# A rotary embedding on one core: batch 0 stored whole, behind all five first loads

## The chip, the cores and the metric

The kernel runs on one core of a Trainium2 chip. The metric is the time of one execution on the device in microseconds (us). It is shown as the median of several executions. One further execution was taken with the hardware profiler on; all durations of single instructions and transfers come from that one.

A core has compute engines that work side by side. This kernel uses three of them for arithmetic or for starting transfers: VectorE (DVE), which does all multiplications and additions; ScalarE (ACT), which does a few conversions; and GpSimd (POOL), which here only issues transfers. SyncE (SP) issues four further transfers. The transfers themselves are moved by 16 DMA engines, which the page sums up as one row. Transfers that POOL issues stand in the queue that the page calls q0 (software_dynamic), those of SP in q1 (hardware_dynamic).

## The reference

The input `x` has 8 batches of 2048 positions, 16 heads and 64 elements, in float32; `cos` and `sin` have 32 values for each position. The two halves of each head are rotated against each other:

```python
def reference(x, cos, sin):
    head_dim = x.shape[-1]                       # 64
    x1 = x[..., :head_dim // 2].copy()
    x2 = x[..., head_dim // 2:].copy()
    cos = cos[None, :, None, :].copy()
    sin = sin[None, :, None, :].copy()
    out1 = x1 * cos - x2 * sin
    out2 = x1 * sin + x2 * cos
    return np.concatenate([out1, out2], axis=-1).astype(np.float32)
```

## The kernel before

A batch is 2048 positions, laid over 128 partitions with J = 16 positions ("rows" below) in each. A row is 16 heads of 64 elements, 1024 in all, so a whole batch is 128 x 16384 elements: 8.39 MB in float32 in main memory, half of that in float16 on the chip. All arithmetic is in float16. The transfers convert: a load reads float32 from main memory and writes float16 to the chip, a store does the reverse. The page gives the sizes of these transfers on the float16 side (4096 KB for a batch).

`buf` (line 47) is one tile with five slots, and batch b lives in slot b % 5, where it is loaded, rotated in place and stored from. So batches 0 to 4 have a slot from the start, and batches 5, 6 and 7 need the slots of 0, 1 and 2, after these have been stored.

`load(b, n)` (lines 62 to 71) issues one transfer for n neighbouring batches. For batch 0 it leaves out the first JA = 2 rows. Those come through the tile `head` in float32, on SP's queue (line 41), and ACT converts them into the slot (line 106). `store(b, n, j0, j1)` (lines 73 to 81) issues one transfer for n batches, or for rows j0 to j1 of one batch. Both are issued by POOL, and `in_ring` (lines 51 to 60) chains them, so that POOL issues them in the order in which the code calls them; it adds no wait of its own. An instruction on POOL that waits, though, holds up all issues behind it.

`rotate(b, j0, j1)` (lines 83 to 100) is three DVE operations over the rows given: the halves swapped times sine into the temporary `v` (L92), the batch times cosine in place (L98), and the sum (L100). A store waits for the L100 of its rows. The first L92 of a batch waits for its load.

SP issues sin_f, head and cos_f at the start (lines 40, 41 and 45). ACT converts sine (two forms, lines 104 and 105), the two head rows (106) and cosine (110).

The order of work around the change: load(0) and load(1) are issued; the first two rows of batch 0 are rotated; row 0 is stored; load(2, 2) for batches 2 and 3, and load(4); the other 14 rows of batch 0 are rotated, and rows 1 to 15 stored; then batches 1 and 2 are rotated and stored one by one, and load(5, 2) and load(7) fill the slots that come free. load(5, 2) waits for the stores of batches 0 and 1, load(7) for that of batch 2. Later stores are store(3, 2), store(5, 2) and batch 7 in three parts, the last of which goes out in float32 through `head` on SP's queue.

Of the kernel before, what the change touches and what calls it, by code (L numbers as in the profile page):

```python
# [1 line left out]

# [4 lines left out]


@with_exitstack  # L10
def kernel(
    ctx: ExitStack,
    tc: tile.TileContext,
    x: bass.AP,
    cos: bass.AP,
    sin: bass.AP,
    out: bass.AP,
):
    nc = tc.nc
    f16 = mybir.dt.float16  # L20
    f32 = mybir.dt.float32

    B, S, H, D = x.shape
    Dh = D // 2
    P = nc.NUM_PARTITIONS
    J = S // P
    NBUF = 5

    const_pool = ctx.enter_context(tc.tile_pool(name="rope_const", bufs=1))
    io_pool = ctx.enter_context(tc.tile_pool(name="rope_io", bufs=1))  # L30
    tmp_pool = ctx.enter_context(tc.tile_pool(name="rope_tmp", bufs=1))

    JA = 2
    head = const_pool.tile([P, JA, H, D], f32)
    x0 = x[0].rearrange("(p j) h d -> p j (h d)", j=J)
    sin_f = const_pool.tile([P, J, Dh], f32)
    cos_f = const_pool.tile([P, J, Dh], f32)
    cos_h = const_pool.tile([P, J, Dh], f16)
    sin_h = const_pool.tile([P, J, D], f16)
    nc.sync.dma_start(out=sin_f, in_=sin.rearrange("(p j) d -> p j d", j=J))  # L40
    nc.sync.dma_start(  # L41
        out=head.rearrange("p j h d -> p (j h d)"),
        in_=x0[:, 0:JA, :].rearrange("p j f -> p (j f)"),
    )
    nc.sync.dma_start(out=cos_f, in_=cos.rearrange("(p j) d -> p j d", j=J))

    buf = io_pool.tile([P, NBUF, J, H, D], f16)

    ring = []

    def in_ring(dma):
        if ring:
            tc.add_manual_dep(
                dma.ins,
                ring[-1].ins.name,
                mybir.DependencyInfo(mybir.DependencyClass.NoSync, mybir.DependencyReason.DATA),
                reason="order of the ring",
            )
        ring.append(dma)
        return dma  # L60

    def load(b, n=1):
        k = b % NBUF
        if n == 1:
            j0 = JA if b == 0 else 0
            dst = buf[:, k, j0:J, :, :].rearrange("p j h d -> p (j h d)")
            src = x[b].rearrange("(p j) h d -> p j (h d)", j=J)[:, j0:J, :].rearrange("p j f -> p (j f)")
        else:
            dst = buf[:, k : k + n, :, :, :].rearrange("p b j h d -> p b (j h d)")
            src = x[b : b + n].rearrange("b (p j) h d -> p b (j h d)", j=J)  # L70
        in_ring(nc.gpsimd.dma_start(out=dst, in_=src))  # L71

    def store(b, n=1, j0=0, j1=J):
        k = b % NBUF
        if n == 1:
            src = buf[:, k, j0:j1, :, :].rearrange("p j h d -> p (j h d)")
            dst = out[b].rearrange("(p j) h d -> p j (h d)", j=J)[:, j0:j1, :].rearrange("p j f -> p (j f)")
        else:
            src = buf[:, k : k + n, :, :, :].rearrange("p b j h d -> p b (j h d)")
            dst = out[b : b + n].rearrange("b (p j) h d -> p b (j h d)", j=J)  # L80
        return in_ring(nc.gpsimd.dma_start(out=dst, in_=src))  # L81

    def rotate(b, j0=0, j1=J):
        v = tmp_pool.tile([P, J, H, D], f16)
        n = j1 - j0
        js = slice(j0, j1)
        xt = buf[:, b % NBUF, js, :, :]
        shape = [P, n, H, 2, Dh]
        sin_b = sin_h[:, js, :].rearrange("p j (e d) -> p j e d", e=2).unsqueeze(2).to_broadcast(shape)
        cos_b = cos_h[:, js, :].unsqueeze(2).to_broadcast([P, n, 2 * H, Dh])  # L90
        xe = xt.rearrange("p j h (e d) -> p j h e d", e=2)
        nc.vector.tensor_mul(  # L92
            out=v[:, js, :, :].rearrange("p j h (e d) -> p j h e d", e=2),
            in0=xe[:, :, :, ::-1, :],
            in1=sin_b,
        )
        xw = xt.rearrange("p j h (e d) -> p j (h e) d", d=Dh)
        nc.vector.tensor_mul(out=xw, in0=xw, in1=cos_b)  # L98
        xa = xt.rearrange("p j h d -> p (j h d)")
        nc.vector.tensor_add(out=xa, in0=xa, in1=v[:, js, :, :].rearrange("p j h d -> p (j h d)"))  # L100

    load(0)
    load(1)
    nc.scalar.copy(out=sin_h[:, :, Dh:D], in_=sin_f)  # L104
    nc.scalar.mul(out=sin_h[:, :, 0:Dh], in_=sin_f, mul=-1.0)  # L105
    nc.scalar.copy(  # L106
        out=buf[:, 0, 0:JA, :, :].rearrange("p j h d -> p (j h d)"),
        in_=head.rearrange("p j h d -> p (j h d)"),
    )
    nc.scalar.copy(out=cos_h, in_=cos_f)  # L110
    rotate(0, 0, JA)
    store(0, 1, 0, 1)
    load(2, 2)
    load(4)
    rotate(0, JA, J)
    store(0, 1, 1, J)
    rotate(1)
    store(1)
    rotate(2)
    store(2)  # L120
    load(5, 2)
    load(7)
    rotate(3)
    rotate(4)
    store(3, 2)
    rotate(5)
    rotate(6)
    store(5, 2)
    rotate(7)
    gate = store(7, 1, 0, 9)  # L130
    store(7, 1, 9, J - JA)
    last = buf[:, 7 % NBUF, J - JA : J, :, :].rearrange("p j h d -> p (j h d)")
    dst = out[B - 1].rearrange("(p j) h d -> p j (h d)", j=J)[:, J - JA : J, :].rearrange("p j f -> p (j f)")
    nc.scalar.copy(out=head.rearrange("p j h d -> p (j h d)"), in_=last)  # L134
    end = nc.sync.dma_start(out=dst, in_=head.rearrange("p j h d -> p (j h d)"))
    tc.add_manual_dep(
        end.ins,
        gate.ins.name,
        mybir.DependencyInfo(mybir.DependencyClass.Sync, mybir.DependencyReason.DATA),
        reason="the last rows go out behind this part",  # L140
    )


# [1 line left out]
_INS = ['x', 'cos', 'sin']  # L145
_OUTS = [((8, 2048, 16, 64), 'float32')]


# [23 lines left out]
```

## Time and profile before

| What | Value |
|---|---|
| median of 3 executions | 316.51 us (316.36 to 316.55) |
| the profiled execution | 316.6 us |
| its span (first to last recorded work) | 314.8 us |
| read from and written to main memory | 67.63 MB and 67.11 MB |
| DVE operation on a whole batch (128 x 16384) | 8.69 us |
| one issue on POOL, one batch / two batches | 0.54 to 0.6 us / 0.71 us |
| sin_f (256 KB), issue to landing | 2.7 us |
| head (1024 KB), issue to landing | 6.9 us |
| cos_f (256 KB), issue to landing | 24.4 us |

The span is cut into 40 equal slices on the page, and each digit of a row is the busy share of a slice in tenths. The same strip can be had for any window, and then a slice is a fortieth of the window. "From issue to landing" runs from the start of the issuing instruction to the completion of the transfer, so it holds the time that the transfer stood in its queue. A row of the table of stretches gives the stretch, its length, the busy time of DVE, ACT and POOL with the number of instructions, the granted TensorE clock (unused here), the share of the DMA engines, and the GB/s that they moved, counted on the side that is written: 200-odd for a load, which writes float16, is as much traffic on the float32 side as 400-odd for a store.

### The profile page before, as it was taken

The page shows a single profiled execution, that of the slowest core. Times are in us where ns is not written, and L with a number is a line of the kernel's source. Part 1 is how long each engine was busy: PE and PEld are TensorE (multiplying, and loading weights), DVE is VectorE, ACT ScalarE, POOL GpSimd, SP SyncE. Part 2 cuts the span into 40 slices and gives each one's busy share as a digit, 9 for nine tenths or more (in the row PEclk, how much of TensorE's full clock was granted, in tenths as well). Part 3 has the DMA queues.
Part 4 walks back from the last instruction along what each step waited for, and adds up shares of the span by engine and source line. Part 5 has one row for each costly group of instructions (what it writes and reads, how often), then busy time and mean ns, then how long its engine had stood idle before and what let it go on. Part 6 is the DMA issues. An engine that isn't in the chain of part 4 may idle for free.

```text
span 314.8 us, 115 instructions
## 1 busy us (share of the span) xinstructions
DVE 209.1 (66%) x27; ACT 6.8 (2%) x6; POOL 8.6 (3%) x18
## 2 busy tenths in 40 slices
DVE  0105999999499999999950000899999999910000
ACT  3200000000000000000000000000000000020000
POOL 1002000000000000000010000000000000010000
DMA  9899999999999899999999999999999999999998
GB/s 284 187 262 200 200 266 200 200 262 204 200 200 317 382 492 407 400 400 533 400 200 208 258 200 200 229 237 333 400 491 441 400 400 525 408 400 400 433 427 339
DMA packets 3104, 101.71 MB, mean 323 GB/s; under 512 B 288, under 2 KB 288, under 8 KB 672
## 3 DMA queue, kind: packets, MB, share of 16 engines
q0 software_dynamic: 2528, 99.09, 98.1%
q1 hardware_dynamic: 576, 2.62, 2.2%
HBM read 67.63 MB, written 67.11 MB: 428 GB/s over the span
## 4 chain that ended last, share of the span: by engine, by line
DVE 66%; another core or an unknown queue 13%; DMA 8%; ACT 1%; issue 0%; SPq 0%; DVEq 0%; ACTq 0%
DVE buf L98 22%; DVE buf L100 22%; DVE v L92 22%; DMA cos_f<-in_cos_dram 8%; ACT head L134 1%; ACT cos_h L110 0%; SPq L41 0%; SPq L40 0%; DVEq L92 0%; ACTq L134 0%
## 5 line engine op out<-in xcount | busy, mean ns | idle before, releaser
L92 DVE TENSOR_TENSOR v<-buf,sin_h 128x16384 f16<-128x16384 f16 (+2 forms) x9 | 69.7, 7744 | 51.4 <-DMA buf<-in_x_dram 41.2
L98 DVE TENSOR_TENSOR buf<-buf,cos_h 128x16384 f16<-128x16384 f16 (+2 forms) x9 | 69.7, 7744 | 15.8 <-ACT cos_h L110 15.5
L100 DVE TENSOR_TENSOR buf<-buf,v 128x16384 f16<-128x16384 f16 (+2 forms) x9 | 69.7, 7744 | 0.3
L81 POOL DMA_DIRECT2D out_dram<-buf x8 | 4.7, 586 | 219.4 <-DVE buf L100 219.4
L134 ACT CAST head<-buf 128x2048 f32<-128x2048 f16 x1 | 1.9, 1898 | 249.9 <-DVE buf L100 249.9
L71 POOL DMA_DIRECT2D buf<-in_x_dram x6 | 3.7, 628 | 49.7 <-DMA out_dram<-buf 48.9
L106 ACT CAST buf<-head 128x2048 f16<-128x2048 f32 x1 | 1.9, 1897 | 3.5 <-DMA head<-in_x_dram 3.5
L104 ACT ACT_TABLE_LOAD x1 | 1.3, 1283 | 0.7 <-PEq L156 0.7
L110 ACT CAST cos_h<-cos_f 128x512 f16<-128x512 f32 x1 | 0.6, 617 | 16.1 <-DMA cos_f<-in_cos_dram 16.1
L104 ACT CAST sin_h<-sin_f 128x512 f16<-128x512 f32 x1 | 0.6, 617 | 1.4 <-DMA sin_f<-in_sin_dram 1.4
L105 ACT ACTIVATE sin_h<-sin_f 128x512 f16<-128x512 f32 x1 | 0.6, 624 | 0.0
L156 POOL MEMSET const-float32-0.0<- 128x1 f32 x1 | 0.1, 100 | 0.2 <-issue 0.2
L156 POOL MEMSET const-bfloat16-1.0<- 128x1 bf16 x1 | 0.1, 103 | 0.0
L156 POOL MEMSET const-float32-1.0<- 128x1 f32 x1 | 0.1, 100 | 0.0
L156 POOL MEMSET const-uint8-127<- 128x1 uint8 x1 | 0.1, 100 | 0.0
## 6 DMA issues: line engine op xcount, KB each, us to landing
buf<-in_x_dram POOLq DMA_DIRECT2D x2, 8192.0 KB, 55.2
buf<-in_x_dram POOLq DMA_DIRECT2D x3, 4096.0 KB, 57.4
out_dram<-buf POOLq DMA_DIRECT2D x1, 7680.0 KB, 68.3
out_dram<-buf POOLq DMA_DIRECT2D x1, 4608.0 KB, 28.6
buf<-in_x_dram POOLq DMA_DIRECT2D x1, 3584.0 KB, 22.3
out_dram<-buf POOLq DMA_DIRECT2D x1, 2560.0 KB, 34.1
head<-in_x_dram SPq DMA_DIRECT2D x1, 1024.0 KB, 6.9
out_dram<-head SPq DMA_DIRECT2D x1, 1024.0 KB, 8.4
```

Source lines behind the costliest of these rows:

```text
L71: in_ring(nc.gpsimd.dma_start(out=dst, in_=src))
L81: return in_ring(nc.gpsimd.dma_start(out=dst, in_=src))
L92: nc.vector.tensor_mul(out=v[:, js, :, :].rearrange("p j h (e d) -> p j h e d", e=2), in0=xe[:, :, :, ::-1, :], in1=sin_b,)
L98: nc.vector.tensor_mul(out=xw, in0=xw, in1=cos_b)
L100: nc.vector.tensor_add(out=xa, in0=xa, in1=v[:, js, :, :].rearrange("p j h d -> p (j h d)"))
L104: nc.scalar.copy(out=sin_h[:, :, Dh:D], in_=sin_f)
L105: nc.scalar.mul(out=sin_h[:, :, 0:Dh], in_=sin_f, mul=-1.0)
L106: nc.scalar.copy(out=buf[:, 0, 0:JA, :, :].rearrange("p j h d -> p (j h d)"), in_=head.rearrange("p j h d -> p (j h d)"),)
L110: nc.scalar.copy(out=cos_h, in_=cos_f)
L134: nc.scalar.copy(out=head.rearrange("p j h d -> p (j h d)"), in_=last)
L156: nc = _bacc.Bacc("TRN2", target_bir_lowering=False, num_devices=1)
```

## The change

Batch 0 is no longer stored in two parts. The store of its row 0 is taken out, the store of rows 1 to 15 becomes one of all 16 rows, and load(2, 2) and load(4) are issued right behind load(0) and load(1). The rotation of batch 0 stays in two parts (two rows, then fourteen).

```diff
@@ -101,6 +101,8 @@
 
     load(0)
     load(1)
+    load(2, 2)
+    load(4)
     nc.scalar.copy(out=sin_h[:, :, Dh:D], in_=sin_f)
     nc.scalar.mul(out=sin_h[:, :, 0:Dh], in_=sin_f, mul=-1.0)
     nc.scalar.copy(
@@ -109,11 +111,8 @@
     )
     nc.scalar.copy(out=cos_h, in_=cos_f)
     rotate(0, 0, JA)
-    store(0, 1, 0, 1)
-    load(2, 2)
-    load(4)
     rotate(0, JA, J)
-    store(0, 1, 1, J)
+    store(0)
     rotate(1)
     store(1)
     rotate(2)
```

POOL's order of issues becomes load(0), load(1), load(2, 2), load(4), store(0), store(1), store(2), load(5, 2) and so on: 13 transfers in place of 14. The order on DVE, ACT and SP is the same. load(5, 2) waits for one store of batch 0 where it waited for two.

## The prediction

> **What bounds the kernel now.** I read the page first: shares of the span, the slices, the queues, the chain of waits.
>
> ```profile
> span 314.8 us, 115 instructions
> DVE 209.1 (66%) x27; ACT 6.8 (2%) x6; POOL 8.6 (3%) x18
> ...
> DMA  9899999999999899999999999999999999999998
> ...
> q0 software_dynamic: 2528, 99.09, 98.1%
> ```
>
> No compute engine fills the span: DVE works 66% of it. The 16 DMA engines are at 8 or 9 tenths in every slice, and one queue, q0, that of POOL's issues, accounts for 98.1% of them. The chain of waits names DVE for 66% only because it walks back from the last cast along DVE; the queue is the bound. So a change is worth what it alters in that queue's time, not what an instruction costs.
>
> How q0 spends its time I read from the DMA issues, one at a time (KB on the f16 side, then us from issue to landing), with start times from the timeline:
>
> ```profile
> buf<-in_x_dram POOLq DMA_DIRECT2D x1, 3584.0 KB, 22.3
> buf<-in_x_dram POOLq DMA_DIRECT2D x1, 4096.0 KB, 41.6
> out_dram<-buf POOLq DMA_DIRECT2D x1, 512.0 KB, 15.2
> buf<-in_x_dram POOLq DMA_DIRECT2D x1, 8192.0 KB, 53.2
> buf<-in_x_dram POOLq DMA_DIRECT2D x1, 4096.0 KB, 71.9
> out_dram<-buf POOLq DMA_DIRECT2D x1, 7680.0 KB, 68.3
> out_dram<-buf POOLq DMA_DIRECT2D x1, 61.4
> ```
>
> They are load(0), load(1), the one-row store, load(2, 2), load(4), the fifteen-row store and store(1), issued at 1.24, about 1.85 (half of 1.21 later), 29.53, 30.06, about 30.8, 52.52 and 78.69 us. Start plus time to landing gives landings at 23.5, 43.5, 44.7, 83.3, 102.7, 120.8 and 140.1. Their order is the order of issue, and the steps are 20.0, 1.2, 38.6, 19.4, 18.1 and 19.3 us: a batch costs the queue 19.3 either way, one row 1.2, and nothing between them. The store issued at 52.52 lies 50 us in the queue before its turn. A transfer's issue time matters only if it comes later than the end of the one ahead.
>
> **The change, part by part.**
>
> *The three issues that move.* load(2, 2) and load(4) go from 30.06 to behind load(1), so to about 2.45. POOL no longer waits 27 us for the first rotation's L100; nothing else is in its queue there. SP and ACT keep their instructions, order and waits. The loads land no earlier for being issued earlier, because load(1) holds the queue until 43.5 in both kernels: 0. The cover is load(0) and load(1), together 42 us of transfers, and without it the price would be the 1.26 us of the two issues.
>
> *The one-row store goes.* Its 0.54 us of issue on POOL is off the path: 0. In the queue it gives back 1.2 (landings 43.5 to 44.7).
>
> *The merged store has a sixteenth row.* Sixteen rows take 19.3 (store(1)) against 18.1 for fifteen: 1.2 taken again. It still waits for the second rotation's L100, at 52.5, and its turn in the queue comes at about 101; so the wait is covered by 48 us, and behind it on POOL stand only store(1), due at 78.7, and store(2). The 128 packets of the row store and its completion packets go; a batch of 8.39 MB on the f32 side in 19.3 us is 435 GB/s, at which a row's 0.52 MB takes 1.2 us by itself, so they have cost nothing that shows: 0 to -0.1.
>
> *What lies around the row store.* Here there is something to gain. I laid windows of 6 us over the change from load(1) to the row store and over the change from load(4) to the fifteen-row store. Bytes are booked where a packet begins, a slice is 0.15 us, and all 16 engines begin a packet within three or four slices:
>
> ```profile
> GB/s 0 0 0 0 0 218 1311 1748 218 0 0 0 0 0 0 0 0 0 0 0 0 0 0 0 55 219 437 410 437 437 437 437 355 1775 1338 655 0 0 0 0
> ```
>
> ```profile
> GB/s 0 0 0 1529 1092 874 0 0 0 0 0 0 0 0 0 0 0 0 0 1639 2458 2048 410 0 0 0 0 0 0 0 0 0 0 0 1638 2458 2048 410 0 0
> ```
>
> The first is 39 to 45 us. load(1)'s last packets begin in the slice of 39.75, the row store's first at 42.6, load(2, 2)'s at 43.95. The second is 99 to 105: load(4)'s last packets at 99.45, the store's first at 101.85. A last load packet ahead of large store packets takes 16 slices, 2.4 us; ahead of the small ones 19 slices, 2.85 us: 0.45 lost (0.15 either way by the slices). The stretch table agrees on the order of it:
>
> ```profile
> 23.00:42.70 19.70, 15.85 (x4) 0.62 (x1) 1.79 (x3) 1.00 1.00 211
> ...
> 44.00:82.60 38.60, 34.26 (x5) 0.00 (x0) 1.08 (x2) 1.00 1.01 217
> ```
>
> 211 GB/s against 217 over 19.7 us is 0.55 us, and load(1)'s landing step is 20.0 against 19.3, 0.7, of which part belongs to the last cos_f packets that come in between. With no small store behind load(1) I expect the 0.45 back. Bounds: 0, if the slow packet has another reason or moves to the next change from load to store, and 0.6, the slices' upper end. I take 0.45, from the row that looks at the packet itself.
>
> *What follows.* load(2, 2) lands some 1.65 us earlier (1.2 + 0.45), at 81.6, so DVE's 4.99 us of waiting there becomes 3.3; that is off the path. From the end of the merged store on, all is 0.45 earlier. Each later issue must still precede the end of the transfer ahead of it: load(5, 2), issued at 140.72 behind store(1)'s landing, with store(2) in the queue until 159.4 (109.82 + 49.6, read like the landings above); store(3, 2) at 162.18 against load(7)'s landing at 217.4; store(5, 2) at 250.69 against store(3, 2)'s at 256.0, the tightest; store(7) at 276.88 against 294.6. The first and the third hang on landings of this same queue, so they move with it and keep their margins.
>
> Sum: -1.2 + 1.2 - 0.45 = -0.45 us on a span of 314.8, that of an execution of 316.6 us (1.8 lies around the span). That execution is 0.1 above the median of 316.51, from which I take it off: 316.1 us, 0.14% less.
>
> **The rivals.**
>
> *Another issue's fixed cost comes off as well (faster).* sin_f, alone in idle queues, takes 2.7 us to land for 0.26 MB, which at 435 GB/s is 0.6, so 2.1 are fixed. If the row store paid them in the queue, one transfer fewer gives 316.5 - 2.1 = 314.4. Against it: the row store's step is 1.2, its bytes alone, and the changes from load(2, 2) to load(4) and from store to store show no gap. The Trainium skill (DMA: Bandwidth & Descriptors, "Anatomy of one DMA — SWDGE (gpsimd) path") fits about 2.0 us plus bytes at 436 GB/s to one DMA and asks to coalesce small ones; by that rule the sum would be 314.5. The trace agrees with it for sin_f and not for a transfer that queues behind another.
>
> *Nothing is regained (no change).* The slow packet belongs to the first change from load to store, whatever follows. Then the sum is 0 to -0.1: 316.5. For it: it is one event. Against it: of the three changes from loads to stores only the one with small packets behind it shows it.
>
> *The queue starts later (slower).* POOL now issues four loads in a row at the start. If load(0)'s first packets are let go only when POOL's run of issues is through, two more issues, 1.26 us, stand ahead of everything, with only the small cos_f to fill the hole: 316.5 - 0.45 + 1.26 = 317.3. The cover is head, whose packets hold the engines until about 5.3:
>
> ```profile
> DMA  9692879999657993991990990990991999999000
> GB/s 184 123 184 82 307 307 430 471 594 594 266 246 328 410 573 164 573 573 82 655 573 0 573 737 0 573 737 0 492 737 82 410 860 655 1434 2007 287 0 0 0
> ```
>
> These are 2 to 6 us: load(0)'s large packets begin at 5.2 to 5.6, where head's end, so they were ready by then; how long before is not shown. It makes the kernel slower by 0.2% from a delay of 1.1 us on (0.45 + 0.63). If the 4.0 us from load(0)'s issue to its first packet grew with the batches queued, five for two, it would be 6.1 us more and 322.2. Against it: the three issues at 29.53 to 31.3 took POOL 0.54 to 0.7 each, as single ones do, so issues in a row don't hold each other up, and load(0) is the first of its queue. The depth is nothing new: five batches queued at 3.8 us, and at 162.9 load(5, 2), load(7) and store(3, 2), five less what load(5, 2) had moved in 3 us.
>
> **How the numbers follow.** The forecast 0.58, nothing regained 0.14, a later start 0.22, the fixed cost 0.06. A measurement of this kernel tells 0.2%, 0.63 us, from no change (the three runs shown lie within 0.19). Faster: 0.06 and 0.09 of the forecast, where more than 0.6 comes back: 0.15. Slower: 0.20 of the later start's 0.22, the rest being too short to count. Within: 0.65. The likeliest has its own range from 315.9 (0.6 back) to 316.5. The whole range goes down to 315.6, for the spread of the measurement below that, and up to 317.4, the later start by the two issues; left out are the fixed cost and a start that is later still.
>
> **What would show it.** Right: 128 row packets and their 16 completions are gone (3104 packets become 2960); load(0) lands at 23.5 as before, load(1) at 43.0, load(2, 2) at 81.6, the merged store's landing 0.45 before 120.8; steps of 19.3 throughout; store(5, 2) issued ahead of store(3, 2)'s landing. Wrong: a hole in the slices at 5.3 us or a load(0) that lands late (the later start); a packet of 2.85 us at the change from load(4) to the merged store (nothing regained); steps below 19.3 for a batch; or a store that POOL issues after the queue has run dry.

## The result, and the profile after

| | median | runs | profiled execution | its span |
|---|---|---|---|---|
| before | 316.52 us (316.30 to 317.66) | 22 | 316.6 us | 314.8 us |
| changed | 317.33 us (317.11 to 317.88) | 22 | 317.18 us | 315.4 us |

The changed kernel takes 1.0024 times as long, with a 95% interval of 1.0018 to 1.0030. It is slower by 0.8 us between the medians and by 0.6 between the two profiled executions. The traces can explain the 0.6. The other 0.2 lies in which executions were profiled: the one before is 0.1 above its median, the changed one 0.15 below. For the runs further down, the ratios leave out executions more than 1.5% above the fastest of their kernel, while the medians hold them.

The page of the changed kernel, in the lines that matter (the span; DVE; the busy tenths of the DMA engines in 40 slices; the packets; the share of POOL's queue):

```profile
span 315.4 us, 114 instructions
...
DVE 209.1 (66%) x27; ACT 6.8 (2%) x6; POOL 8.1 (3%) x17
...
DMA  9899999999999999999999999999999999999998
...
DMA packets 2960, 101.71 MB, mean 322 GB/s; under 512 B 272, under 2 KB 272, under 8 KB 528
...
q0 software_dynamic: 2384, 99.09, 98.0%
```

The same bytes are moved in 144 packets fewer (128 of the row store, 16 completions), DVE does the same work, and the DMA engines are as full as before. So the queue still bounds the kernel, and it has become longer.

The DMA issues of the changed kernel, one at a time (KB on the float16 side, us from issue to landing), say where:

```profile
buf<-in_x_dram POOLq DMA_DIRECT2D x1, 3584.0 KB, 22.4
buf<-in_x_dram POOLq DMA_DIRECT2D x1, 4096.0 KB, 41.1
buf<-in_x_dram POOLq DMA_DIRECT2D x1, 8192.0 KB, 79.2
buf<-in_x_dram POOLq DMA_DIRECT2D x1, 4096.0 KB, 98.8
out_dram<-buf POOLq DMA_DIRECT2D x1, 68.8
out_dram<-buf POOLq DMA_DIRECT2D x1, 62.0
```

They are load(0), load(1), load(2, 2), load(4), store(0) and store(1), issued at 1.24, about 1.9, 2.5, 3.2, 52.54 and 78.72 us. They land at 23.6, 43.0, 81.7, 102.0, 121.3 and 140.7. The steps behind load(0) are 19.4, 38.7, 20.3, 19.3 and 19.4. One of them is a microsecond too long: load(4), the last load ahead of the first store. The strip of 97 to 103 us (0.15 us a slice, bytes booked where a packet begins) shows the place:

```profile
GB/s 0 0 0 0 0 874 1092 1311 218 0 0 0 0 0 0 0 0 0 0 0 0 0 0 0 0 0 0 0 2185 1311 2622 874 0 0 0 0 0 0 0 0
```

load(4)'s last packets begin from the slice of 97.75 on, the store's first from that of 101.2: 23 slices instead of 16. In the packet records of the trace (start and duration of each packet), the 16 engines take 1.02 us more than the usual 2.43 for their last packet of load(4), as a mean. The load packet at the turn behind load(1), which took 0.39 us more in the kernel before, is normal now, there being no turn. So 0.4 came back, and 1.0 was lost 55 us later. Two rows of the table of stretches (us, DVE, ACT and POOL busy, clock, DMA share, GB/s) agree: load(4) has 206 GB/s over 20.35 us where the loads before it have 217, and at 217 it would take 1.0 us less.

```profile
42.20:80.90 38.70, 36.09 (x5) 0.00 (x0) 1.08 (x2) 1.00 1.01 217
80.90:101.25 20.35, 19.44 (x3) 0.00 (x0) 0.00 (x0) 1.00 1.01 206
```

### The profile page after: what moved, and what is told of

Read it like the earlier page. It is cut to its first block, busy times and chain, and to the rows that moved or that the text cites. A ratio compares the mean times of both kernels' runs of the same rounds, so it can differ in the third digit from the quotient of the medians.

```text
span 315.4 us, 114 instructions
## 1 busy us (share of the span) xinstructions
DVE 209.1 (66%) x27; ACT 6.8 (2%) x6; POOL 8.1 (3%) x17
## 4 chain that ended last, share of the span: by engine, by line
DVE 66%; another core or an unknown queue 13%; DMA 8%; ACT 1%; issue 0%; SPq 0%; DVEq 0%; ACTq 0%
DVE buf L98 22%; DVE buf L100 22%; DVE v L92 22%; DMA cos_f<-in_cos_dram 8%; ACT head L133 1%; ACT cos_h L112 0%; SPq L41 0%; SPq L40 0%; DVEq L92 0%; ACTq L133 0%
```

## The experiments

In what follows "the turn" is the point at which the queue goes from loads to stores, "the wait" is what the last load packet at a turn takes beyond 2.43 us, as a mean over the 16 engines from the packet records, and "the small store" is what is stored ahead of the bulk of batch 0. Bytes per engine are counted on the chip's side: one float16 row is 2 KB in each of 8 partitions, 16 KB per engine. Comparisons are with runs of the kernel before on the same chip. Changes against the kernel before or the changed kernel are given as diffs. They are shortened: `...`, and words in parentheses, stand for code left out. `part(h0, h1)` is one transfer on POOL's queue that stores heads h0 to h1 of the 256 (16 rows of 16) that each partition has of batch 0.

### Place, size and issue time

**The row store behind all five loads (against the changed kernel).**

```diff
-    rotate(0, JA, J)
-    store(0)
+    store(0, 1, 0, 1)
+    rotate(0, JA, J)
+    store(0, 1, 1, J)
```

> All five loads at once, then the one-row store, then the fifteen-row store. Theory A (the first store of the run makes the engines wait once, 0.45 us with packets of one row, 1.0 us with packets of sixteen): load(4)'s last packets take about 2.85 us, nothing else is slow, total as before, 316.5 us. Theory B (five loads queued from the start make the turn from loads to stores dear, whatever store comes first): last packets stay at about 3.45 us, total 317.3.

The wait is 1.08 us at the turn, in front of packets of one row. The median is 317.98 us, ratio 1.0045 (1.0029 to 1.0061). Theory A in its first form, that small packets make the wait small, fails. What differs from the kernel before is that further stores, not a load, stand behind the row. Theory B would fit this run.

**The loads held back (against the changed kernel).** load(2, 2) waits for the first rotation.

```diff
     load(1)
-    load(2, 2)
-    load(4)
...
     rotate(0, 0, JA)
+    load(2, 2)      # with a wait for the last L100 of this rotation
+    load(4)
```

> The changed kernel, but load(2, 2) and load(4) are held back by a wait until the first two rows are rotated (about 29 us), as they were before; batch 0 still leaves as one store. Theory A: nothing changes against the changed kernel, last packets of load(4) at about 3.45 us, total 317.3. Theory B (issue time and depth of the queue): the slow packets are gone, total 316.1.

The wait is 1.02 us at the turn, as in the changed kernel. The median is 317.59, ratio 1.0018 (0.9994 to 1.0042). The interval holds 1.0, the time of the kernel before, but not the 0.998 of theory B's 316.1 us. The profiled execution took 326 us, and in it the two loads were issued at 48.72 us, not at about 29; the last section comes back to it. The packets of a run further down, row 0 of 16 partitions, decide: there both loads are issued at 29.99 us, as before the change, and the wait behind load(4) is 1.20 us. Theory B falls, since issuing the loads late does not spare the wait.

**Two rows in the small store (against the kernel before).**

```diff
-    store(0, 1, 0, 1)
+    store(0, 1, 0, JA)
...
-    store(0, 1, 1, J)
+    store(0, 1, JA, J)
```

> The kernel before, with two rows in the small store between load(1) and load(2, 2) and fourteen in the large one. Theory A with a cost that grows with the packet: load(1)'s last packets take more than the 2.85 us of one row, by up to 0.1 us for one row more; total 316.5 to 316.6. Theory A with a cost that has only two sizes, or that hangs on the place: 2.85 or 3.45 us.

The wait behind load(1) is 0.94 us and none is left behind load(4). The median is 317.28, ratio 1.0029 (1.0003 to 1.0054). With one row more, the wait is nearly as long as before sixteen. The size of the small store matters.

**A touch of out's memory (against the changed kernel).** Sixteen pieces of 256 B, copied from x to out at the start, on ACT's queue.

```diff
+    nc.scalar.dma_start(out=out[0, 0:16, 0, :], in_=x[0, 0:16, 0, :])
```

> The changed kernel with one tiny transfer more at the very start, on ACT's queue: 16 pieces of 256 B copied from x to the head of out, which the store of batch 0 writes over later. Theory A1 (the wait is for the first touch of out's memory): load(4)'s last packets fall to 2.43 us, total 1.0 us under the changed kernel, about 316.3. Theory A2 (the wait belongs to the first store from the chip's memory, or the first with this conversion, on POOL's queue): they stay at about 3.45 us, total 317.3.

The wait stays, at 1.09 us. The median is 317.38, ratio 1.0027 (1.0017 to 1.0038). The first touch of the output is not what costs.

### Once, and by what amount

**The row store one load later (against the kernel before).**

```diff
-    store(0, 1, 0, 1)
     load(2, 2)
+    store(0, 1, 0, 1)
     load(4)
```

> The kernel before, with the one-row store moved one load on: load(0), load(1), load(2, 2), the one-row store, load(4). Theory C (the first store of the run makes all engines wait once; the wait is cut short to 0.4 us where only one row per partition is stored and a load follows): batch 3's last load packets, at about 80 us, are 0.4 us longer, total as before, 316.5. Theory D (the wait grows with the time that has passed or the packets that went ahead, 0.4 at 43 us and 1.0 at 100 us): about 0.8 us longer, total 316.9 or more.

The wait is 0.30 us behind batch 3 (80 us), and there is none behind load(4). The median is 316.69, ratio 1.0000 (0.9983 to 1.0017). Theory D, which had about 0.8 us there, falls.

**A second one-row store (against the kernel before).**

```diff
     load(2, 2)
+    store(0, 1, 1, 2)
     load(4)
...
-    store(0, 1, 1, J)
+    store(0, 1, 2, J)
```

> The kernel before, with row 1 stored by itself as well, between load(2, 2) and load(4). Theory C (once in a run): load(1)'s last packets 0.4 us longer as before, batch 3's last packets at 2.43 us; total as before, 316.5. Rival (every small store between loads makes the engines wait): both 0.4 us longer, total 316.9.

The wait is 0.39 us at the first small store, 0.00 at the second, and there is none behind load(4). The median is 316.50, ratio 0.9994 (0.9978 to 1.0010). It is paid once. A later turn, from load(7) to store(3, 2), shows 0.00 in every profile of this document. This is also a second profile with the kernel before's order up to 80 us, with the same 0.39.

**Half a row (against the kernel before).**

```diff
-    store(0, 1, 0, 1)
+    part(0, 8)       # heads 0 to 7 of row 0
...
-    store(0, 1, 1, J)
+    part(8, J * H)   # the rest of batch 0
```

> The kernel before, with half a row in the small store and fifteen and a half in the large one. Theory C with a wait that goes by the bytes of the first store (0.4 us for one row, 0.94 for two, no more than 1.05 for more): load(1)'s last packets are some 0.2 us longer, total 316.3. A wait that does not go by bytes: 0.4 or 1.0 us, total 316.5 to 317.1.

Behind load(1) the wait is only 0.07 us. But now the store of the rest makes load(4)'s last packets 0.50 us longer, where after a whole row nothing was left. Its strip of 97 to 103 us has 19 slices from packet to packet, between the 16 of the kernel before and the 23 of the changed one:

```profile
GB/s 0 0 0 0 0 0 0 0 0 0 1092 1311 1092 0 0 0 0 0 0 0 0 0 0 0 0 0 0 0 0 1693 1693 2116 1270 0 0 0 0 0 0 0
```

The median is 316.68, ratio 0.9995 (0.9960 to 1.0031).

**A tiny store first (against the changed kernel).** 2 KB per engine, out of a tile of zeros, on POOL's queue ahead of load(0).

```diff
+    warm = const_pool.tile([P, 2 * D], f16)
+    nc.gpsimd.memset(warm, 0.0)
+    in_ring(nc.gpsimd.dma_start(out=..., in_=warm))   # 256 B of each partition, into batch 0
     load(0)
```

> The changed kernel with one tiny store first of all on POOL's queue: 128 pieces of 256 B, f16, out of a tile of zeros into the head of out's rows, converted as the others are and written over later by the store of batch 0. Theory A2 or C (the first store from the chip's memory on this queue pays, once): load(4)'s last packets, at 98 us, fall to 2.43 us; the wait is paid near 5 us, hidden or shorter; total 316.1 to 316.6. Rival (the turn from loads to large stores pays wherever it is first): they stay at 3.45 us, total 317.3 or more.

A wait of 0.86 us is left behind load(4). The median is 317.28, ratio 1.0023 (1.0003 to 1.0042). So the wait left was 1.02, 0.86, 0.50 and 0.00 us behind 0, 2, 8 and 16 KB per engine. These fit two readings: bytes, or the share of each 4 KB of out that has been met.

### Bytes, addresses or queue

**Larger pieces by another queue (against the changed kernel).**

```diff
+    nc.scalar.dma_start(out=out[0, 0:16] ..., in_=x[0, 0:16] ...)   # 16 pieces of 4 KB
```

> The changed kernel with a copy from x to out on ACT's queue at the very start, as in the touch of 256 B pieces, but 16 pieces of 4 KB, one for each engine. So far the wait left for the first large store was 0.86 us behind 512 B per partition (written side), 0.5 behind 2 KB, none behind 4 KB. Theory E (what has to be met once are the addresses of out within a 4 KB step, such as the channels of the memory): 4 KB pieces from any queue meet all of them, load(4)'s last packets fall to 2.43 us, total 316.1 to 316.4. Theory F (what counts are the bytes stored before, 32 KB per engine, or that they come from the chip's memory over POOL's queue): 0.9 to 1.0 us left, total 317.3.

A wait of 1.09 us is left. The median is 317.48, ratio 1.0025 (1.0015 to 1.0035).

**Row 0 of 16 partitions (against the kernel before).**

```diff
-    store(0, 1, 0, 1)
+    (row 0 of partitions 0 to 15)
...
-    store(0, 1, 1, J)
+    store(0)
```

> The kernel before, but the small store between load(1) and load(2, 2) takes row 0 of 16 partitions alone (16 pieces of 4 KB on the written side, one for each engine, an eighth of the bytes), and batch 0 then leaves whole, row 0 of these partitions a second time. Theory E: hardly any wait behind load(1), none behind load(4); total 316.1 to 316.3, less than before. Theory F (bytes): 0.9 us left behind load(4), total 317.0 to 317.3.

There is no wait behind load(1), and one of 1.20 us behind load(4). The median is 317.32, ratio 1.0016 (1.0002 to 1.0029). The strip of 97 to 103 us has 24 slices from load(4)'s last packets to the store's first:

```profile
GB/s 0 0 0 0 0 0 874 874 1529 218 0 0 0 0 0 0 0 0 0 0 0 0 0 0 0 0 0 0 0 0 874 2622 2185 1311 0 0 0 0 0 0
```

**The tiny store in 4 KB pieces (against the changed kernel).** As the tiny store first, from 16 partitions.

```diff
+    (memset of 16 x 1024 in slot 4 of buf, stored to row 0 of partitions 0 to 15)
     load(0)
```

> The changed kernel with a store of zeros first on POOL's queue, as the one of 128 pieces of 512 B (written side), with the same 64 KB in 16 pieces of 4 KB, out of a free slot of buf; written over later. Theory E: load(4)'s last packets at 2.43 us, total 316.1 to 316.6. Theory F: 0.86 us left as behind the pieces of 512 B, total 317.3.

A wait of 0.79 us is left. The median is 317.44, ratio 1.0026 (1.0016 to 1.0036). All three speak against theory E: meeting every address within 4 KB does not spare the wait. That agrees with theory F, in which the dose is what counts.

**Half the partitions (against the kernel before).** As row 0 of 16 partitions, with 64.

```diff
-    store(0, 1, 0, 1)
+    (row 0 of partitions 0 to 63)
...
-    store(0, 1, 1, J)
+    store(0)
```

> The kernel before with row 0 of 64 partitions in the small store (four pieces of 4 KB for each engine, half the bytes) and batch 0 stored whole later. Theory F: as with the half row of all partitions, 0.1 us behind load(1) and 0.5 behind load(4); total 317.1 with 0.6 us of transfers more. Rival (pieces of 4 KB are enough): none left behind load(4), total 316.7. Rival (all eight pieces of an engine are needed): 1.0 left, 317.6.

The wait is 0.00 us behind load(1) and 0.47 behind load(4). The median is 317.34, ratio 1.0025 (1.0016 to 1.0035). Four pieces of an engine, 2 KB each on the chip's side, act as the eight pieces of 1 KB did: what counts is the bytes, not the number of pieces.

**The row sent elsewhere (against the kernel before).**

```diff
-    store(0, 1, 0, 1)
+    (the same row, to row 0 of batch 7 in out)
...
-    store(0, 1, 1, J)
+    store(0)
```

> The kernel before with its one-row store sent to row 0 of batch 7 in out (written over later), and batch 0 stored whole, so 1.2 us more of transfers. If the addresses in out matter: 1.0 us left behind load(4), total 318.7. If they do not: load(4)'s last packets at 2.43 us, 0.4 behind load(1) as before, total 317.7.

The wait is 0.33 us behind load(1), and there is none behind load(4): a row sent to another place in out spares the wait as well. The median is 317.98, ratio 1.0040 (1.0026 to 1.0053), with 1.2 us of transfers more.

**The same bytes by SP's queue (against the changed kernel).**

```diff
+    nc.sync.dma_start(out=(row 0 of batch 0), in_=head[:, 0, :, :] ...)   # float32, unrotated
     nc.scalar.copy(out=cos_h, in_=cos_f)
```

> The changed kernel with a row's bytes (0.5 MB, 4 KB per partition) stored early by SP's queue, float32 to float32 out of head, unrotated, to row 0 of batch 0, which the whole store writes over. It adds 1.2 us of transfers. If writing these bytes to out from any queue spares the wait: load(4)'s last packets at 2.43 us, total 317.3 - 1.0 + 1.2 to 1.6 = 317.5 to 317.9. If only POOL's queue or the conversion counts: 1.0 us left, total 318.5 to 318.9.

A wait of 0.96 us is left. The median is 318.54, ratio 1.0060 (1.0047 to 1.0074). The strips of 97 to 103 us of these last two, the row sent elsewhere first, then SP's queue:

```profile
GB/s 1748 1092 0 0 0 0 0 0 0 0 0 0 0 0 0 437 1966 1092 0 0 0 0 0 0 0 0 0 0 0 0 0 874 3059 2622 437 0 0 0 0 0
```

```profile
GB/s 874 437 218 0 0 0 0 0 0 0 0 0 0 0 437 1529 874 437 0 218 0 0 0 0 0 0 0 0 0 0 0 0 0 0 0 0 0 2622 1311 2622
```

From the group of load(4)'s last packets to the store's first there are 16 slices in the one and 23 in the other. The run differs from a row on POOL's queue in one more thing than the queue: SP's packets of 4 KB went in singly between load packets, from 25.5 us on, and not in one block.

**POOL's queue without conversion (against the changed kernel).**

```diff
     load(1)
+    in_ring(nc.gpsimd.dma_start(out=(row 0 of batch 0), in_=head[:, 0, :, :] ...))   # float32
     load(2, 2)
```

> The changed kernel with a row's bytes stored between load(1) and load(2, 2) on POOL's queue, but without conversion, float32 out of head (unrotated, written over by the whole store). If the queue counts: load(4)'s last packets at 2.43 us, up to 0.4 us behind load(1); total 317.3 - 1.0 + 1.2 to 1.6 = 317.5 to 317.9. If the conversion counts: 0.9 to 1.0 us left behind load(4), total 318.5 or more.

The wait is 0.89 us behind load(1) and 0.00 behind load(4). The median is 318.41, ratio 1.0056 (1.0041 to 1.0071). The strip of 39 to 45 us has 22 slices from load(1)'s last packets to the small store's first:

```profile
GB/s 0 0 0 0 0 0 1966 1092 218 218 0 0 0 0 0 0 0 0 0 0 0 0 0 0 0 0 0 0 219 355 382 382 437 437 437 437 1338 1447 901 218
```

A store without conversion spares the later wait too, if it goes as one block on POOL's queue; no run sent one block by SP's queue. The 0.89 is not the 0.39 of the float16 row, which writes as many bytes, but close to the 0.94 of two rows, which read as many: 32 KB per engine. So the amount seems to go by the bytes read on the chip, not by those written. As this run changes the conversion along with the bytes read, that rests on this one comparison.

### Two half doses

**With a load between them (against the kernel before).**

```diff
-    store(0, 1, 0, 1)
+    part(0, 8)
     load(2, 2)
+    part(8, 16)
     load(4)
```

> The kernel before, with row 0 stored in two halves: one between load(1) and load(2, 2) as the half row before, one between load(2, 2) and load(4), then rows 1 to 15. Theory F (the wait left at the first large store goes down with the bytes stored before, and a small dose costs little by itself): 0.06 to 0.15 us at each half, none at the fifteen rows, total 0.2 to 0.3 us under the kernel before, 316.3. Rival (a store has to have a whole row per partition to help): 0.5 us left behind load(4), total 316.7 or more.

No wait is left at any of the three turns: 0.01, 0.00 and 0.00 us. The median is 316.40 against 316.66, ratio 0.9986 (0.9971 to 1.0001). The strips of 39 to 45 and of 97 to 103 us:

```profile
GB/s 0 0 0 0 0 655 1092 1092 437 218 0 0 0 0 0 0 0 0 0 0 0 27 137 314 369 423 1161 1857 505 451 0 0 0 0 0 0 0 0 0 0
```

```profile
GB/s 437 218 0 0 0 0 0 0 0 0 0 0 0 437 874 1529 218 437 0 0 0 0 0 0 0 0 0 0 0 0 1639 3687 410 819 0 0 0 0 0 0
```

The step from load(1)'s last packets to the small store is 16 slices, from load(4)'s to the fifteen rows 16 from peak to peak. The last packet of the run ends at 313.4 us, before the 313.6 of the kernel before and the 314.2 of the changed one.

**The same once more.** The kernel is the one just shown.

> The kernel with two half rows once more, unchanged. If its gain is real: no packet over 2.5 us at the turns, end of the queue 0.25 us before that of the kernel before, total 0.2 to 0.3 us under it (ratio 0.9991 to 0.9994). If the first time was chance: a wait at one of the turns, total as before.

The waits are 0.03, 0.00 and 0.00 us, and the last packet ends at 313.3. The median is 316.36 against 316.60. The ratio is 0.9998 (0.9985 to 1.0011). Twice the median is 0.25 us lower and twice the trace shows the same 0.2 to 0.3, but neither interval leaves 1.0 out, so a gain over the kernel before is likely and not established. Both intervals lie below that of the changed kernel (1.0018 to 1.0030), whose 317.33 is about 0.95 us more.

**Both halves at one place (against the kernel before).**

```diff
-    store(0, 1, 0, 1)
+    part(0, 8)
+    part(8, 16)
     load(2, 2)
```

> The kernel before with its one-row store split into two halves that stand one behind the other, both between load(1) and load(2, 2). If the load between the doses is what spares the wait: load(1)'s last packets 0.4 us longer, as with the one-row store, total 316.5 to 316.7. If small transfers spare it: under 0.15 us, total 316.3 to 316.4.

The wait is 0.41 us behind load(1), and there is none later. The median is 316.67, ratio 1.0001 (0.9992 to 1.0010). So what lets the two doses pass free is the load between them, or the 38 us that it takes, and not that each transfer is small.

### What the runs add up to

| Read on the chip, per engine, by stores ahead of the first large one | wait at the small store | wait left at the large store |
|---|---|---|
| nothing (changed kernel; loads held back; two touches from x) | | 1.02; 1.02; 1.09; 1.09 us |
| 2 KB, three forms | 0.00 at the one between loads | 0.79 to 1.20 |
| 8 KB, two forms | 0.00 and 0.07 | 0.47 and 0.50 |
| 16 KB (kernel before; at 80 us; elsewhere in out; halves together) | 0.39; 0.30; 0.33; 0.41 | 0.00 |
| 16 KB with the other rows right behind (row store behind all five loads) | 1.08 | |
| 16 KB in two doses with a load between | 0.01 and 0.00 | 0.00 |
| 32 KB (two rows; float32 row) | 0.94; 0.89 | 0.00 |
| 32 KB on SP's queue | | 0.96 |

Each figure is one profile. The wait is paid once in a run, by the first stores on POOL's queue. About 16 KB read per engine, with a load behind them, are enough to settle it. A dose of up to 8 KB between loads costs next to nothing, one of 16 KB 0.3 to 0.4 us, and one of 32 KB or more the whole, about 1.0. What 2 KB spare is not settled: 0.79 to 1.20 lies on both sides of the 1.02 to 1.09 without any dose. What happens inside an engine during the wait was not seen, so its own cause stays open.

## Why the prediction was wrong

**The bound was right.** DMA engines full in every slice, POOL's queue the limit, 19.3 us for a batch either way: the changed kernel shows steps of 19.3 and 19.4 everywhere but at the turn.

**The moved issues cost nothing, as said.** load(0) lands at 23.6 us against 23.5 and its packets begin behind head's; load(2, 2) lands at 81.7, forecast at 81.6. DVE's wait for it fell from 4.99 to 3.32 us. store(5, 2) was still in time.

**The row store and the sixteenth row cancelled, as said.** store(0) takes 19.3, and 144 packets are gone.

**The step that failed is "What lies around the row store".** Its term was -0.45 us, with 0 as the worst bound; the runs show -0.39 and +1.02. It read the slow packet rightly, 0.45 by slices and 0.39 by the packet records, and rightly tied it to the row store; the 0.4 did come back. It failed in what it set as the bound on the other side, 0 if the packet "moves to the next change from load to store". It did move, and at 1.02 us instead of 0.39. In the sum, -0.4 + 1.0 is +0.6, which is what the spans show (315.4 against 314.8) and the ends of the queue (314.2 against 313.6).

The view that misled was the turn from load(4) to the fifteen-row store in the kernel before. Its 16 slices were taken to show that a turn in front of large packets is free. They showed a turn at which the wait had been paid already, by the row store 55 us earlier. "Only the one with small packets behind it shows it" was true, but that one was also the first of the run. The rival "nothing is regained" named just this ("belongs to the first change from load to store, whatever follows") and was given 0.14; it too let the cost keep its size. A bound for it could not be read from a trace in which the first turn is the only one that pays.

**The rival that gave the measured time was wrong.** "The queue starts later" came to 317.3 us, and 317.33 was measured. But the first packets of load(0) begin at 5.3 us in both kernels, and the four issues in a row took POOL 2.47 us without holding the first. The number agreed by chance. **The fixed cost of a transfer** was not regained either: there is one transfer fewer, and no step is shorter by 2 us. The 2.1 us had been read from sin_f, which SP issues and which stands behind no other transfer.

## What to carry to other kernels

A boundary in a trace that costs nothing may do so because an earlier one has paid: compare the first of a kind with the first, not with a later one. A small transfer that looks like overhead can carry a one-time cost at a place where it is cheaper; before it is merged, look at what is longer just beside it and ask what will be the first in its stead. Where a queue that bounds a kernel runs loads only for long, one or two small stores between them, here 8 KB per engine each, can cost less than a large first store: about 1 us of 317 in this kernel with two of them.

## What had not been expected of the hardware

The one-time wait itself was not expected. It is 1.02 us, as a mean of the 16 engines, at the first large store on POOL's queue. A block of 16 KB per engine stored on the same queue between earlier loads spares it, in both places of out that were tried. 32 KB stored by SP's queue, singly between load packets, did not.

The second surprise stands in the profiled execution with the loads held back. In the profile of the kernel before, load(0)'s first packet begins at 5.28 us, when 127 of head's 128 packets have begun. Here it began at 4.68, when 86 had, and the others went in between the packets of load(0), the last at 22.35:

```profile
head<-in_x_dram SPq DMA_DIRECT2D x1, 1024.0 KB, 23.9
```

```profile
45.94 1.23 DVE L98 TENSOR_TENSOR buf<-buf,cos_h 128x2048 f16<-128x2048 f16 x1 [17.66 <-ACT cos_h L110]
47.20 1.23 DVE L100 TENSOR_TENSOR buf<-buf,v 128x2048 f16<-128x2048 f16 x1
48.46 7.62 DVE L92 TENSOR_TENSOR v<-buf,sin_h 128x14336 f16<-128x14336 f16 x1
48.72 1.25 POOL L71 DMA_DIRECT2D buf<-in_x_dram  x2 [46.27 <-DVE buf L100]
```

```profile
DMA  2099209920200000000000099200990099009900
```

head took 23.9 us to land instead of 6.9, and cos_f 43.6 instead of 24.4. The first rotation ended at 48.4 instead of 29.2, and the held loads were issued at 48.72, after load(1) had ended. The last line is the strip of 36 to 60 us (0.6 us a slice, packets booked where they begin): from 42.6 to 49.8 no packet begins, and the execution took 326 us.

The run with a touch of out's memory had nearly the same start: load(0) began at 3.93 us, when 49 of head's packets had begun, head took 22.7, and the first rotation ended at 47.0. But its five loads were all queued from the start, and the same strip has no hole:

```profile
DMA  2099209920992099209920992099209920992099
```

That execution took 318.47 us. In the kernel before, the row store holds load(2, 2) and load(4) back behind the first rotation in the same way as in the execution of 326 us. Its profile shows no such hole, and no further execution of it was profiled, so whether it meets one was not seen.
